# Stacked 128-row score products and single-pass sums of squares in the differential attention of a two-layer encoder

## The chip, the cores and the metric

The kernel runs on one core of one Trainium2 chip. The metric is the device time of one execution in microseconds (us). Three runs of the kernel before the change took 2218.12, 2219.3 and 2221.23 us; their median is 2219.3 us.

The engines are TensorE (PE, with its weight loads listed as PEld), VectorE (DVE), ScalarE (ACT), GpSimd (POOL) and SyncE (SP). In this kernel every data transfer is issued from SP's queue.

## What is computed

Two layers of an encoder over 512 tokens of width 1024. Each layer projects its input once and feeds three branches (a bidirectional state-space scan, differential attention, cross-attention into 256 memory tokens), gates and merges them, projects them out and normalizes. The change is in the differential attention, of which the reference says:

```python
q = _apply_rope(dq.reshape(Bsz, S, DIFF_HEADS, 2, DIFF_HEAD_DIM), cos, sin)
k = _apply_rope(dk.reshape(Bsz, S, DIFF_HEADS, 2, DIFF_HEAD_DIM), cos, sin)
...
s = jnp.einsum('bqhcd,bkhcd->bhcqk', qblk, k) * scale
p = jax.nn.softmax(s.astype(jnp.float32), axis=-1)
w = p[:, :, 0] - lam * p[:, :, 1]
return jnp.einsum('bhqk,bkhe->bqhe', w, vf)
...
o = _rmsnorm(o, diff_norm_w[layer]) * (1.0 - lambda_init)
```

There are 8 heads. Each head has two maps c of 64 channels, so a head's 128 rows of query (or key) hold map 0 in rows 0 to 63 and map 1 in rows 64 to 127. The norm at the end needs, for each token and head, the sum of squares of 128 output channels.

## The kernel before

All large products are made in float32r, a single-pass format, from operands split into a high part and a low part: `split` (line 93) copies x to the high part on ACT and subtracts it from x on DVE for the low part, and `mm3` (line 105) adds three products, low times high, high times low and high times high. Products that are given plain float32 take two passes each in the trace.

Weights come in units of 128 x 1024 (512 KB, `wr`), each loaded by one DMA and split by ACT and DVE (`emit`, line 131), two units ahead of their use. The tile framework schedules the instructions of all engines but, in the differential attention, PE: `diff` (line 793) opens a manual schedule for PE at line 984, so PE's order is the order of the text.

`diff` builds a list of units, one projection each, and lays one step per unit (lines 988 to 1016). For each head h the units are: the query of head h+1, the key of head h+1 (both `rope`, line 819), and two of the gate (`gpart`) or value (`vpart`) projections. Step s also holds, ahead of the unit's first half, the scores of query chunk s+1 (`scores`, line 873; 4 chunks of 128 tokens per head, 32 per layer) and, between the halves, the products with the values for a pair of chunks (`values`, line 907) and the turning of chunk s's weights (`turn`, line 897). In steps with s % 4 == 1 the sums of squares of the head before (`sums`, line 921) follow the scores. So a head's key is projected in the step s = 4h+1, and the first scores that read it stand at the start of step 4h+3, one step between them. The units of head 0 come before that loop; the first scores stand in the middle of `vpart(1)`.

`rope` reads the projection out of PSUM on ACT (`rx`), makes a copy with 32-row halves swapped by four DMAs of 32 rows (`rsw`, line 828), multiplies by cosine and sine and adds on DVE, and splits the result into two tiles of 128 x 512, high and low, which hold both maps.

`scores` makes three products per map on the 64 rows of that map (lines 884 to 887), the maps alternating, into two PSUM banks; DVE takes the row minimum (`fmx`; the query carries a negative scale), ACT the exponential (`fpp`).

`sums` multiplies each 128-token chunk of the squares (`sq`, float32, tile `fth`) as weights by a column of ones, four products of one column, and ACT copies the four columns to the table `ss`, tokens in rows. `norm` (line 927) makes the factors of all heads but the last after step 29, and those of the last head after step 33; `spread` and `last` distribute them, `fin` applies them and splits the result into `dy`, the operand of the branch projection. `wout` (line 1036) reuses tiles of the same pool by their tags.

## Time and profile before

One execution was profiled. It took 2223.68 us, around a span of 2221.9 us from its first to its last instruction; the mean granted TensorE clock was 0.997.

| engine | busy us | share of the span | instructions |
|---|---|---|---|
| PE | 2171.0 | 98% | 11330 |
| PEld | 1768.0 | 80% | 11330 |
| DVE | 1585.9 | 71% | 2440 |
| ACT | 1004.3 | 45% | 1895 |
| POOL | 54.2 | 2% | 38 |

A line of a timeline gives the start in us from the span's start, the duration in us, the engine, the line of the code, the operation, the tiles written and read, the shape of the array and of the operand, and the count; in brackets, how long the engine was idle before it and what it waited for. Because helpers such as `mm`, `act` and `tt` record the operations, many share a line (103, 91, 81), and the tile names tell them apart. `pm<-k,q` are the score products, `pt<-cst,fth` the sums of squares, `pj<-...` projections. A matmul is shown from its start to its modelled end; matmuls overlap, so the distance between starts is what one costs in a stream. In the list of DMAs a line gives the count, the size of each and the median time from issue to landing. The chain of waits lists, back from the last instruction, what each step waited for; its lines give start, duration and the group of instructions.

### The profile page before, as it was taken

Reading aid. Unit: us, or ns where it says so; the run is one execution under the profiler, and the core shown is the slowest. Engines: PE = TensorE matmul, PEld = TensorE weight load, DVE = VectorE, ACT = ScalarE, POOL = GpSimd, SP = SyncE. Lnnn points to the kernel's source line nnn. Section 1 sums busy time; section 2 is a strip of 40 time slices with the busy share of each in tenths; the row PEclk is TensorE's granted clock in tenths of the full one; section 3 lists DMA queues with packets and bytes.
Section 4 is the critical chain, followed back from the end, with each engine's and each line's share of the span. In section 5 each row is a group of like instructions: output and inputs, shape, how many; then the busy total and the mean of one; then the engine's idle time right before and its main releaser. Section 6 shows DMA issues by size and latency. Waiting matters only on the chain.

```text
span 2221.9 us, 29523 instructions
## 1 busy us (share of the span) xinstructions
PE 2171.0 (98%) x11330; PEld 1768.0 (80%) x11330; DVE 1585.9 (71%) x2440; ACT 1004.3 (45%) x1895; POOL 54.2 (2%) x38
## 2 busy tenths in 40 slices
PE   8999999999999999999999999999999999999998
PEld 6787877788887888878887777777788887888786
DVE  7887878758554777766467888888754547777567
ACT  5664545424442454543355564545423324554440
POOL 0000000000000000000000100000100000000000
PEclk9999999999999999999999999999999999999999
DMA  4654554425553322224564654454434333222353
GB/s 149 182 160 144 144 136 144 125 86 167 168 173 117 95 85 79 77 89 147 152 214 122 177 146 145 133 152 132 124 105 132 105 113 94 75 84 81 91 154 112
DMA packets 106162, 283.73 MB, mean 128 GB/s; under 512 B 12524, under 2 KB 13092, under 8 KB 105764
## 3 DMA queue, kind: packets, MB, share of 16 engines
q1 hardware_dynamic: 106020, 281.84, 42.4%
q8 instruction: 89, 1.46, 0.3%
q14 instruction: 53, 0.43, 0.1%
HBM read 255.55 MB, written 17.85 MB: 123 GB/s over the span
## 4 chain that ended last, share of the span: by engine, by line
PE 71%; DVE 14%; DMA 8%; ACT 5%; issue 1%; POOL 0%; SPq 0%; POOLq 0%; DVEq 0%; ACTq 0%
PE pj L103 55%; PE pm L103 13%; DMA ab<-dab 5%; DVE wl L81 3%; PE pt L111 2%; DVE ab L81 2%; DVE acc L84 2%; ACT ab L91 1%; ACT wh L91 1%; DMA wr<-wu 1%; DVE y L81 1%; DVE rx L81 1%; PE pt L103 1%; DMA fth<-rd 1%; DVE m L81 1%
## 5 line engine op out<-in xcount | busy, mean ns | idle before, releaser
L103 PE MATMUL pj<-xh,wl 128*128 128x512 f32 x1664 | 669.2, 402 | 11.0 <-DVE wl L81 8.9
L103 PE MATMUL pj<-xh,wh 128*128 128x512 f32 x1664 | 661.0, 397 | 0.0
L103 PE MATMUL pj<-xl,wh 128*128 128x512 f32 x1664 | 658.5, 396 | 0.0
L81 DVE TENSOR_TENSOR wl<-wr,wh 128x1024 fp32r<-128x1024 f32 x330 | 405.7, 1230 | 109.0 <-ACT wh L91 108.1
L91 ACT ACTIVATE wh<-wr 128x1024 fp32r<-128x1024 f32 x330 | 347.4, 1053 | 228.4 <-PE pj L103 147.4
L103 PEld LDWEIGHTS pj<-xh,wl 128*128 128x128 f32 x1664 | 313.9, 189 | 91.2 <-issue 18.3
L103 PEld LDWEIGHTS pj<-xh,wh 128*128 128x128 f32 x1664 | 313.8, 189 | 71.7 <-issue 5.7
L103 PEld LDWEIGHTS pj<-xl,wh 128*128 128x128 f32 x1664 | 314.2, 189 | 63.6 <-issue 3.6
L91 ACT ACTIVATE ab<-ab,bias 128x128 f32<-128x128 f32 x512 | 160.8, 391 | 120.5 <-DVE ab L81 119.7
L84 DVE SCALAR_TENSOR_TENSOR acc<-pj,hcw,acc 128x510 f32<-128x510 f32 x192 | 142.4, 744 | 24.2 <-ACT acc L91 22.8
L91 ACT ACTIVATE fpp<-pm,fmx 128x512 f32<-128x512 f32 x128 | 87.9, 687 | 84.3 <-DVE fmx L889 83.6
L889 DVE TENSOR_REDUCE fmx<-pm 128x1 f32<-128x512 f32 x128 | 87.0, 686 | 45.9 <-PE pm L103 45.5
L103 PE MATMUL pj<-yl,wh 128*128 128x512 f32 x256 | 102.4, 400 | 0.9 <-DVE yl L84 0.9
L103 PE MATMUL pj<-yh,wh 128*128 128x512 f32 x256 | 103.0, 403 | 0.0
L81 DVE TENSOR_TENSOR ab<-ab,cst 128x1024 f32<-128x1024 f32 x64 | 85.4, 1334 | 24.4 <-DMA ab<-dab 24.4
L103 PE MATMUL pj<-dy,wh 128*128 128x512 f32 (+1 forms) x384 | 102.2, 354 | 0.1
L103 PE MATMUL pj<-yh,wl 128*128 128x512 f32 x256 | 102.0, 399 | 0.0
L103 PE MATMUL pj<-cy,wh 128*128 128x512 f32 x256 | 78.8, 389 | 0.0
L103 PEld LDWEIGHTS pj<-dy,wh 128*128 128x128 f32 x384 | 67.8, 189 | 11.0 <-DVE dy L81 0.9
L103 PE MATMUL pj<-wh,xl 128*128 128x256 f32 x256 | 74.8, 292 | 0.0
L81 POOL TENSOR_TENSOR sqa<-sqa,sz 128x512 f32<-128x512 f32 x32 | 52.9, 1654 | 845.6 <-ACT sz L91 845.6
L103 PE MATMUL pj<-wl,xh 128*128 128x256 f32 x256 | 72.4, 283 | 0.0
(273 smaller groups left out, 3269.1 us busy)
## 6 DMA issues: line engine op xcount, KB each, us to landing
wr<-wu SPq DMA_DIRECT2D x336, 512.0 KB, 3.7
ab<-dab SPq DMA_DIRECT2D x64, 512.0 KB, 5.7
eb<-deb SPq DMA_DIRECT2D x64, 256.0 KB, 4.7
mkv<-dkv SPq DMA_DIRECT2D x16, 512.0 KB, 4.5
rsw<-rx SPq DMA_DIRECT2D x128, 64.0 KB, 2.0
dgt<-tg SPq DMA_DIRECT2D x18, 256.0 KB, 2.8
dkv<-mo SPq DMA_DIRECT2D x16, 256.0 KB, 4.2
dkv<-q SPq DMA_DIRECT2D x16, 256.0 KB, 3.6
```

What stands on the lines that cost most here:

```text
L81: (eng or self.nc.vector).tensor_tensor(out=out, in0=a, in1=b, op=op)
L84: self.nc.vector.scalar_tensor_tensor(out=out, in0=a, scalar=s, in1=b, op0=op0, op1=op1)
L91: self.nc.scalar.activation(out=out, in_=a, func=f, **kw)
L103: self.nc.tensor.matmul(out=out, lhsT=a, rhs=b, start=first, stop=last)
L111: self.nc.tensor.transpose(out=out, in_=x, identity=self.ident)
L889: nc.vector.tensor_reduce(out=mx[:, c:c + 1], in_=ps, axis=AX.X, op=ALU.min)
```

## The change

Query and key are no longer kept as high and low tiles with both maps. After the split, high and low of a head go into one tile `hl` (tag `qkh`), and DMAs lay them out anew. For the key, one tile per map holds the 64 high rows above the 64 low rows: four DMAs of 64 x 512 (128 KB). For the query, each map has a high and a low tile, each with its 64 rows twice, in both halves: four DMAs of 64 x 1024 (256 KB) into slots of a tile `qst`, two heads in turn. A score map is then two products over 128 rows, low query times key stack and high query times key stack, four per chunk in place of six over 64 rows. They include the product of both low parts, which the kernel before leaves out.

For the sums, the squares are split into high and low (tile `sqs`). Two products with weights `pick` of 8 columns, whose column h is ones for head h and zero otherwise, give a result of 8 x 512 with the sums in row h, which DVE adds to `sr`. Before each `norm`, a new step `flip` turns the four chunks of `sr` with four transposes and copies the heads needed to `ss`.

To find room, `qst` and `sqs` take the slots of `dy`, which is allocated anew in a step `room` after step 32; some tags of `wout` change with it. A constant of 64 columns is added.

```diff
+            hl = self.t(fp, [P, 2, S], "qkh", F32R)
+            self.split(hl[:, 0, :], hl[:, 1, :], x)
+            half = [slice(64 * c, 64 * c + 64) for c in range(2)]
+            if nm == "q":
+                o = [self.qst[:, 4 * (h % 2) + 2 * c:4 * (h % 2) + 2 * c + 2, :] for c in range(2)]
+                self.qk[h, nm] = [[t[:, i, :] for i in range(2)] for t in o]
+                parts = [(o[c][r], hl[half[c]]) for c in range(2) for r in half]
+            else:
+                o = self.qk[h, nm] = [self.t(fp, [P, S], f"k{c}", F32R) for c in range(2)]
+                parts = [(o[c][half[i], :], hl[half[c], i, :]) for c in range(2) for i in range(2)]
+            for to, src in parts:
+                nc.sync.dma_start(out=to.bitcast(F32), in_=src.bitcast(F32))
...
-            for n, (a, b) in enumerate(((ql, kh), (qh, kl), (qh, kh))):
-                for c in range(2):
-                    rows = slice(64 * c, 64 * c + 64)
-                    self.mm(pss[c], a[rows, qs], b[rows, :], n == 0, n == 2)
+            for c in range(2):
+                (qh, ql), k = self.qk[h, "q"][c], self.qk[h, "k"][c]
+                self.mm(pss[c], ql[:, qs], k, True, False)
+                self.mm(pss[c], qh[:, qs], k, False, True)
...
-                self.sq = self.t(self.fp, [P, S], "fth")
-                self.act(self.sq, po, AF.Square)
+                sq = self.t(self.fp, [P, S], "fth")
+                self.act(sq, po, AF.Square)
+                self.sq = [self.sqs[h % 2][:, i, :] for i in range(2)]
+                self.split(*self.sq, sq)
...
         def sums(h):
             pt = self.bank(self.pt, "pt")
+            for i in (1, 0):
+                self.mm(pt[:KC], self.pick[:, h, :], self.sq[i], i == 1, i == 0)
+            if h == 0:
+                self.act(self.sr, pt[:KC])
+            else:
+                self.tt(self.sr, self.sr, pt[:KC], ALU.add)
+
+        def flip(lo, hi):
+
+            pt = self.bank(self.pt, "pt")
             for c in range(4):
-                self.mm(pt[:, c:c + 1], self.sq[:, c * P:(c + 1) * P], self.ones[:, 0:1])
-            self.act(self.ss[:, 4 * h:4 * h + 4], pt[:, 0:4])
+                nc.tensor.transpose(out=pt[:, c * KC:(c + 1) * KC], in_=self.sr[:, c * P:(c + 1) * P],
+                                    identity=self.ident[:KC, :KC])
+            self.act(self.ss[:, 4 * lo:4 * hi].rearrange("p (h c) -> p h c", c=4),
+                     pt[:, :4 * KC].rearrange("p (c h) -> p h c", c=4)[:, lo:hi])
...
             if s in (nst - 3, nst + 1):
+                self.T(job(flip, *((0, KC - 1) if s < nst else (KC - 1, KC))))
                 self.T(job(norm, *((0, KC - 1) if s < nst else (KC - 1, KC))))
+            if s == nst:
+                self.T(room)
```

## The prediction

> **What bounds the kernel now.** I read the page first: the engines' busy time, then the chain of work that ended last.

> ```profile
> PE 2171.0 (98%) x11330; PEld 1768.0 (80%) x11330; DVE 1585.9 (71%) x2440; ACT 1004.3 (45%) x1895; POOL 54.2 (2%) x38
> PE 71%; DVE 14%; DMA 8%; ACT 5%; issue 1%; POOL 0%; SPq 0%; POOLq 0%; DVEq 0%; ACTq 0%
> ```

> TensorE (PE) is busy nearly all the time and carries 71% of the chain, so PE time removed shows in the total wherever nothing else is late. The change sits in the differential-attention stage, where the chain leaves PE once per head. The timeline of one such place, the key of head 3 in layer 0, with the DMA queue's own lines:

> ```profile
> 818.71 0.60 ACT L91 ACTIVATE rx<-pj 128x512 f32<-128x512 f32 x1 [2.16 <-PE pj L103]
> 819.33 2.41 SPq L828 DMA_DIRECT2D rsw<-rx  x4
> 821.42 0.68 DVE L81 TENSOR_TENSOR q<-rx,q 128x512 fp32r<-128x512 f32 x1
> 823.95 0.68 DVE L81 TENSOR_TENSOR rx<-rx,cos 128x512 f32<-128x512 f32 x1
> 826.53 0.63 ACT L91 ACTIVATE k<-rx 128x512 fp32r<-128x512 f32 x1 [1.50 <-DVE rx L81]
> 826.79 0.39 PE L103 MATMUL pj<-xh,wh 128*128 128x512 f32 x1
> 827.19 0.69 DVE L81 TENSOR_TENSOR k<-rx,k 128x512 fp32r<-128x512 f32 x1
> 827.94 0.73 PE L103 MATMUL pm<-k,q 64*128 64x512 f32 x4 [0.22 <-DVE k L81]
> 828.60 0.51 PE L103 MATMUL pj<-xh,wl 128*128 128x512 f32 x1
> ```

> The projection of the key ends, ACT reads it out at 818.71, the half-swap goes through DMA from 819.33, VectorE (DVE) rotates it, ACT and DVE split it into high and low at 826.53 and 827.19. The score products of the next head wait for that: DVE is done at 827.19 + 0.69 = 827.88, four of the six products start at 827.94. PE is already the one that waits: from 826.79 to 828.60 are 1.81 us, where a block that doesn't wait (below) has 1.22, so 0.6. There is no slack behind the key's split: whatever is put between the split and the products delays PE by its full length.

> **The score products themselves.** A block whose operands are there, on PE's timeline:

> ```profile
> 834.23 0.39 PE L103 MATMUL pj<-xl,wh 128*128 128x512 f32 x1
> 834.45 0.39 PE L103 MATMUL pj<-xh,wh 128*128 128x512 f32 x1
> 834.77 0.97 PE L103 MATMUL pm<-k,q 64*128 64x512 f32 x6
> 835.67 0.50 PE L103 MATMUL pj<-xh,wl 128*128 128x512 f32 x1
> 836.00 0.40 PE L103 MATMUL pj<-xl,wh 128*128 128x512 f32 x1
> ```

> Full products follow each other every 0.23 us (834.23 to 834.45). From the last one before the block (834.45) to the second one behind it (836.00) are 1.55 us, of which two steps of 0.23 would pass anyway: the block costs 1.09 us. Six products of 0.23 would be 1.38, so the two 64-row halves do run beside each other in pairs, and entering and leaving that form eats part of the gain. The new block is four full products, 4 x 0.23 = 0.92 us: 0.17 saved. Not the third that a count of six against four suggests.

> Of the 64 blocks, 16 are the first of a head and are costed with the stall below. In 14 intervals (heads 1 to 7, two layers) one more block lies between the end of the key's projection and the stalled products; time saved there only lengthens the wait, as the key's chain starts at the projection's end. That leaves 34 x 0.17 = 5.8 us.

> **The sums of squares.**

> ```profile
> 810.34 0.39 PE L103 MATMUL pj<-xh,wh 128*128 128x512 f32 x1
> 810.66 0.96 PE L103 MATMUL pm<-k,q 64*128 64x512 f32 x6
> 811.55 1.05 PE L103 MATMUL pt<-cst,fth 128*128 128x1 f32 x8
> 812.46 0.48 PE L103 MATMUL pj<-xh,wl 128*128 128x512 f32 x1
> 812.78 0.39 PE L103 MATMUL pj<-xl,wh 128*128 128x512 f32 x1
> ```

> Each of the four full-precision products makes two passes (8 records). From 810.34 to 812.78 are 2.44 us; less 0.46 and the block of 1.09, the sums take 0.89. Their replacement is two products of 512 columns with 8 weight columns. Nothing that narrow is in the trace; the nearest has 64 weight columns:

> ```profile
> 26.99 0.39 PE L103 MATMUL pj<-xh,wh 128*128 128x512 f32 x1
> 27.21 0.40 PE L103 MATMUL pj<-xh,yl 128*64 128x512 f32 x1
> 27.45 0.39 PE L103 MATMUL pj<-xl,yl 128*64 128x512 f32 x1
> ```

> It enters at the normal step (0.22, 0.24), so I take 0.46 for the two: 0.43 saved. If entering and leaving cost what the score block pays beyond its three pairs (1.09 - 0.69 = 0.40), nothing is saved. 16 heads: -6.9 us, between 0 and -6.9.

> The flips are new: four calls, each with four small transposes. A group of four costs this in the chain:

> ```profile
> 782.66 0.44 PE pt L111 x4
> ```

> 4 x 0.44 = +1.8 us. They come a step after the sums, with half a step left before their result is used.

> New work on ACT and DVE: per head a split of the squares (0.63 and 0.69, the sizes of the key's split above) and an addition of 8 rows by 512 columns on DVE, at most the 0.69 of a 128-row one, in place of a small copy on ACT. It falls into the two steps with the longest waits for PE:

> ```profile
> 810.76 0.60 ACT L91 ACTIVATE rx<-pj 128x512 f32<-128x512 f32 x1 [2.13 <-PE pj L103]
> 811.65 0.69 DVE L889 TENSOR_REDUCE fmx<-pm 128x1 f32<-128x512 f32 x1 [2.13 <-PE pm L103]
> ```

> Idle times of 2.13 us on both cover it: nothing. Were that cover gone, DVE's 1.38 us per head would come to 22 us.

> **The stacking, which is the price.** Products over 128 rows need high and low of one map above each other, that is, data moved across partitions. Per head the change adds four DMAs of 128 KB behind the key's split and four of 256 KB behind the query's, all in SP's queue.

> ```profile
> L828 SPq DMA_DIRECT2D rsw<-rx x128: 507/588/598, 721.8 to 2056.4; - x128
> wr<-wu SPq DMA_DIRECT2D x336, 512.0 KB, 3.7
> eb<-deb SPq DMA_DIRECT2D x64, 256.0 KB, 4.7
> rsw<-rx SPq DMA_DIRECT2D x128, 64.0 KB, 2.0
> dab<-eb SPq DMA_DIRECT2D x2, 128.0 KB, 3.1
> ```

> Issue: 0.59 us each, as the swap. Landing of 128 KB: 2.0 us is the swap's (SBUF to SBUF, half the bytes), 3.1 that of 64 rows of 2 KB to DRAM (the same bytes); far ends are 2.0 and, for 256 KB, 4.7. I take the middle of the two near rows, 2.55.

> For head 3: the first part (high, map 0) needs only ACT's half and goes at 827.16; the second (low, map 0) waits for DVE and goes at 827.88, the third at 828.47, the fourth at 829.06, and lands at 831.61. Map 0's two products run meanwhile; map 1's two take 0.46, and the projection goes on at 832.07 where it went on at 828.60: +3.47 us per head. Behind the waiting products on PE stand all projections, in an order written by hand, so nothing fills the hole.

> The first head of a layer has more room before its products, yet they too start as the split ends:

> ```profile
> 734.64 0.69 DVE L81 TENSOR_TENSOR k<-rx,k 128x512 fp32r<-128x512 f32 x1
> 735.20 0.92 PE pm L103 x6
> 736.12 3.07 PE pj L103 x24
> ```

> The split ends at 735.33, the fourth part goes at 736.51 and lands at 739.06; +0.46 is 739.52 against 736.12: +3.4. Sum: 14 x 3.47 + 2 x 3.4 = +55.4 us.

> The query's parts wait for its split (821.42 + 0.68 = 822.10), hold SP until 824.5 and are due only with the key's: they cost nothing beside it, unless their 1 MB is still moving when the key's parts go (then the 4.7 end). Next weights were asked for before them, two steps ahead of use. [...]

> **Sum.** 55.4 - 5.8 - 6.9 + 1.8 = +44.5 us. The profiled execution took 2223.7 us around its span of 2221.9 (so 2268.2 by the same profile); the median of the runs is 2219.3, hence **2263.8 us**.

> **The rivals.**

> *Hidden (faster).* The key could be stacked in time if its chain started earlier. What is to be had: the swap's last part, issued at about 821.1, has landed by 823.1 and its product waits in DVE's order until 823.95; between that and the split stand other DVE operations of some 1.4 us. Even 2.2 us recovered and a landing of 2.0 leave 3.47 - 0.55 - 2.2 = 0.7 us per head, 11.5 in all, against 10.9 saved (5.8 + 6.9 - 1.8): the sign turns only below 0.7 us per head. Fully hidden, with today's waits of 0.6 gone as well, 2219.3 - 10.9 - 14 x 0.17 - 14 x 0.6 gives 2198. Chance 0.08; against it speaks that the parts' own issue and landing are longer than all of this slack.

> *The query's parts ahead of the key's swap.* In the program the query's stacking stands before the key's swap. If SP keeps that order, the swap goes at 824.5 instead of 819.33, some 5 us later, and so does the key: 14 x 5 more, about 2334. Against it: the swap was ready at 819.33, the query's split ended at 822.10, and ACT already does the key's readout (818.71) ahead of the query's split. Chance 0.1.

> *The slow clock.* After a long wait PE runs at half pace for a while:

> ```profile
> 6.89 0.77 PE L103 MATMUL pj<-xh,wl 128*128 128x512 f32 x1 [6.89 <-DVE wl L81]
> 10.55 0.43 PE L103 MATMUL pj<-xh,wh 128*128 128x512 f32 x1
> 15.70 0.50 PE L103 MATMUL pj<-xh,wl 128*128 128x512 f32 x1 [1.30 <-DVE wl L81]
> 16.04 0.39 PE L103 MATMUL pj<-xl,wh 128*128 128x512 f32 x1
> ```

> Behind 6.89 us of waiting, eight steps took 3.66 us instead of 1.84; behind 1.30 us none was slow. The new hole is 827.02 (826.79 + 0.23) to 830.43, when map 0's second part lands: 3.4 us, between the two. If it counts as long, 16 x 1.8 = +29 us: 2293. [...] Chance 0.2.

> *Nothing.* A stall of just 0.7 us per head would cancel the savings: 2219, chance 0.04.

> **How the numbers follow.** My case, 0.58; clock 0.2; query first 0.1; hidden 0.08; nothing 0.04. With a landing of 2.0 and 1.5 us of DVE's slack recovered the stall is 1.4 us and the time 2231; with 4.7 it is 5.6 and the time 2298; with a landing of 3.95 and the clock's price on top, 2315. The range is 2228 to 2315: it leaves out hidden, nothing and most of query first. Within 0.2% is about what a measurement can tell from no change. Faster 0.08, same 0.04, slower 0.88.

> **What would show it.** In the profile after: score products of 128 rows in blocks of 0.92 us; ahead of the first block of each head PE idle of about 3 us put down to the DMAs of the key's stack, and some 55 us of such waits in all; sums in 0.46 us; the swap still issued ahead of the query's parts; projections behind the hole at steps of 0.23 (mine) or 0.46 (clock). Waits of PE on the key's DMAs below 1 us per head would prove me wrong, and point to DVE's order.

## The result and the profile after

The changed kernel takes 2301.35 us, the median of four runs (2299.27 to 2303.7), against 2218.71 us for the kernel before on the same chip (2217.99 to 2221.23). The ratio is 1.0371, with a 95% interval of 1.0356 to 1.0387: slower by 82.6 us, where the prediction said 44.5. The profiled execution took 2303.7 us, and its mean granted clock was 0.975 (before: 0.997).

From the page after: the busy times, the group of the score products (busy time, mean ns of one | idle time before them and what ended most of it), and the DMAs of the key's parts (KB each, median us from issue to landing).

```profile
PE 2198.6 (96%) x11122; PEld 1807.1 (79%) x11122; DVE 1609.8 (70%) x2470; ACT 1007.7 (44%) x1903; POOL 52.7 (2%) x38
L103 PE MATMUL pm<-k,dy 128*128 128x512 f32 x256 | 87.0, 461 | 60.6 <-DMA k<-qkh 59.7
k<-qkh SPq DMA_DIRECT2D x64, 128.0 KB, 2.5
```

PE has 208 instructions fewer, and yet it is busy 27.6 us longer: some of what it does goes at a slower pace. And it now stands idle for 59.7 us ahead of score products whose key stack has not landed. The next fence shows where: the timeline of after at the key of head 3 in layer 0, the place that the prediction showed of before.

```profile
831.36 2.41 SPq L836 DMA_DIRECT2D rsw<-rx  x4
834.29 3.13 SPq L853 DMA_DIRECT2D dy<-qkh  x4
838.67 0.39 PE L103 MATMUL pj<-xh,wh 128*128 128x512 f32 x1
838.94 0.63 ACT L91 ACTIVATE qkh<-rx 128x512 fp32r<-128x512 f32 x1 [2.02 <-DVE rx L81]
839.59 2.46 SPq L853 DMA_DIRECT2D k<-qkh  x4
842.62 1.19 PE L103 MATMUL pm<-k,dy 128*128 128x512 f32 x2 [3.56 <-DMA k<-qkh]
843.99 1.19 PE L103 MATMUL pm<-k,dy 128*128 128x512 f32 x2 [0.18 <-issue]
844.98 0.63 PE L103 MATMUL pj<-xh,wl 128*128 128x512 f32 x1
845.40 0.63 PE L103 MATMUL pj<-xl,wh 128*128 128x512 f32 x1
...
848.34 0.39 PE L103 MATMUL pj<-xh,wh 128*128 128x512 f32 x1
```

The last projection product starts at 838.67; the next one that isn't a score product starts at 844.98. Less one step of 0.23 that is a span of 6.08 us; the same place of before had 1.58. In it: the split, four issues in 2.46 us, the wait of 3.56 us, and four products at about half pace (the last two take 0.99 us, 843.99 to 844.98, in place of 0.46). Behind it eight projection steps go at up to 0.43 us (844.98 to 845.40 is one; all eight, to 848.34, take 3.36 us, where eight steps of 0.23 are 1.84) before the pace returns.

The first head of a layer has it worse. First the DMA queue's lines and the products of layer 0, then the key's parts in the DMA view of 724 to 738 us:

```profile
726.71 3.52 SPq L853 DMA_DIRECT2D dy<-qkh  x4
730.36 3.78 SPq L853 DMA_DIRECT2D k<-qkh  x4
737.30 2.37 PE L103 MATMUL pm<-k,dy 128*128 128x512 f32 x4 [5.75 <-DMA k<-qkh]
```

```profile
k<-qkh SPq DMA_DIRECT2D x4, 128.0 KB, 5.0
```

Here the query's 1 MB leaves just ahead of the key's parts, both move at once (in this view the query's four parts, issued from 726.71 to 730.23, take 6.3 us to land), and the key's take 5.0 us to land instead of 2.5. The same view has two weight units of 512 KB under way; which of the two loads slows the key's parts isn't separated. The 3.78 us of the four issues hold a wait: the first part goes 1.66 us ahead of the second, which needs DVE's half of the split.

A block that waits for nothing, with the sums behind it:

```profile
860.79 1.09 PE L103 MATMUL pm<-k,dy 128*128 128x512 f32 x4
861.72 0.62 PE L103 MATMUL pt<-dy,pick 128*8 128x512 f32 x2
862.17 0.39 PE L103 MATMUL pj<-xh,wl 128*128 128x512 f32 x1
862.40 0.40 PE L103 MATMUL pj<-xl,wh 128*128 128x512 f32 x1
```

The block takes 0.93 us (860.79 to 861.72), the sums 0.45 (to 862.17), and the step behind is the normal one. So both products became cheaper on PE, as meant.

The loss lies in the differential attention. From the first readout of a query to the issue of the write of the first seven heads' factors (`rd<-rt`) it took 269.0 and 268.9 us in the two layers; now 308.9 and 309.6, together +80.6.

### The profile page after: what moved, and what is told of

Read it like the earlier page. It is cut to its first block, busy times and chain, and to the rows that moved or that the text cites. A ratio compares the mean times of both kernels' runs of the same rounds, so it can differ in the third digit from the quotient of the medians.

```text
span 2301.9 us, 29444 instructions
## 1 busy us (share of the span) xinstructions
PE 2198.6 (96%) x11122; PEld 1807.1 (79%) x11122; DVE 1609.8 (70%) x2470; ACT 1007.7 (44%) x1903; POOL 52.7 (2%) x38
## 3 DMA queue, kind: packets, MB, share of 16 engines
q8 instruction: 87, 1.43, 0.3%
## 5 line engine op out<-in xcount | busy, mean ns | idle before, releaser
L103 PE MATMUL pj<-xh,wl 128*128 128x512 f32 x1664 | 668.8, 402 | 10.2 <-DVE wl L81 8.5
L103 PE MATMUL pj<-xh,wh 128*128 128x512 f32 x1664 | 665.3, 400 | 0.0
L103 PE MATMUL pj<-xl,wh 128*128 128x512 f32 x1664 | 663.6, 399 | 0.0
L81 DVE TENSOR_TENSOR wl<-wr,wh 128x1024 fp32r<-128x1024 f32 x330 | 404.4, 1226 | 107.7 <-ACT wh L91 107.2
L91 ACT ACTIVATE wh<-wr 128x1024 fp32r<-128x1024 f32 x330 | 347.2, 1053 | 222.5 <-PE pj L103 149.6
L103 PEld LDWEIGHTS pj<-xh,wl 128*128 128x128 f32 x1664 | 317.4, 191 | 82.3 <-ACT xh L91 7.0
L103 PEld LDWEIGHTS pj<-xh,wh 128*128 128x128 f32 x1664 | 316.7, 190 | 72.2 <-issue 5.7
L103 PEld LDWEIGHTS pj<-xl,wh 128*128 128x128 f32 x1664 | 317.3, 191 | 67.1 <-issue 3.6
L91 ACT ACTIVATE ab<-ab,bias 128x128 f32<-128x128 f32 x512 | 160.7, 391 | 115.0 <-DVE ab L81 114.1
L103 PE MATMUL pm<-k,dy 128*128 128x512 f32 x256 | 87.0, 461 | 60.6 <-DMA k<-qkh 59.7
L91 ACT ACTIVATE fpp<-pm,fmx 128x512 f32<-128x512 f32 x128 | 87.3, 686 | 92.2 <-DVE fmx L906 92.0
L103 PEld LDWEIGHTS pm<-k,dy 128*128 128x128 f32 x256 | 50.3, 213 | 81.0 <-issue 45.3
L103 PE MATMUL pj<-yl,wh 128*128 128x512 f32 x256 | 102.8, 402 | 0.8 <-DVE yl L84 0.8
L103 PE MATMUL pj<-dy,wh 128*128 128x512 f32 (+1 forms) x384 | 102.7, 356 | 1.0 <-DVE dy L81 1.0
L103 PE MATMUL pj<-yh,wh 128*128 128x512 f32 x256 | 103.2, 403 | 0.0
L103 PE MATMUL pj<-yh,wl 128*128 128x512 f32 x256 | 102.7, 402 | 0.0
L81 DVE TENSOR_TENSOR ab<-ab,cst 128x1024 f32<-128x1024 f32 x64 | 86.7, 1355 | 19.7 <-DMA ab<-dab 19.6
L103 PE MATMUL pj<-wh,xl 128*128 128x256 f32 x256 | 79.1, 309 | 0.0
L103 PE MATMUL pj<-cy,wh 128*128 128x512 f32 x256 | 78.8, 389 | 0.0
L103 PEld LDWEIGHTS pj<-dy,wh 128*128 128x128 f32 x384 | 67.5, 188 | 13.4 <-DVE dy L81 2.3
## 6 DMA issues: line engine op xcount, KB each, us to landing
wr<-wu SPq DMA_DIRECT2D x336, 512.0 KB, 3.7
ab<-dab SPq DMA_DIRECT2D x64, 512.0 KB, 5.3
eb<-deb SPq DMA_DIRECT2D x64, 256.0 KB, 4.9
dy<-qkh SPq DMA_DIRECT2D x64, 256.0 KB, 4.1
mkv<-dkv SPq DMA_DIRECT2D x16, 512.0 KB, 4.2
k<-qkh SPq DMA_DIRECT2D x64, 128.0 KB, 2.5
dgt<-tg SPq DMA_DIRECT2D x18, 256.0 KB, 2.8
```

Source lines behind the costliest of these rows:

```text
L81: (eng or self.nc.vector).tensor_tensor(out=out, in0=a, in1=b, op=op)
L91: self.nc.scalar.activation(out=out, in_=a, func=f, **kw)
L103: self.nc.tensor.matmul(out=out, lhsT=a, rhs=b, start=first, stop=last)
```

## The experiments

Theory A, the prediction's: the stack is late, so PE waits once per head; each hole costs what the split, the issues and the landing add. Theory B adds the slow clock: behind a hole of this length PE runs at half pace for some steps. Of the parts of the change, the sums were held to be a small gain, and the work on ACT and DVE free.

### One part alone

`s1_sums_only` has the new sums and the old scores and rotation:

```diff
-                (qh, ql), k = self.qk[h, "q"][c], self.qk[h, "k"][c]
-                self.mm(pss[c], ql[:, qs], k, True, False)
-                self.mm(pss[c], qh[:, qs], k, False, True)
+            for n, (a, b) in enumerate(((ql, kh), (qh, kl), (qh, kh))):
+                for c in range(2):
+                    rows = slice(64 * c, 64 * c + 64)
+                    self.mm(pss[c], a[rows, qs], b[rows, :], n == 0, n == 2)
```

> The kernel before with the new sums of squares alone (split squares, two products of 512 columns per head, flip); score products as before. My theory: two products at 0.23 us for the 0.89 us of the four double-pass ones, 16 heads, plus four flips of 0.44: 2218.7 - 6.9 + 1.8 = 2213.6 us. Rival, entering and leaving the 8-column form costs what the score block pays (0.40): 2218 to 2221. Rival, the split and the addition on ACT and DVE are not covered: up to 22 us more, 2236. Then a part of the 82 us would lie here.

Measured: 2232.12 us, 1.005 of before (1.0038 to 1.0063). A miss: +11 instead of -5, and inside the bounds of the last rival, that the split and the addition are not covered. Of the profiled run's +8.6, the two stages hold +3.9 (270.9 us each against 269.0 and 268.9); the rest lies in stages that the change doesn't touch, where small waits come and go between profiles, and I give it no cause. Inside the stage the sums do cost PE half of what they did, but the span of the first block now is longer at heads 2 to 7 (2.25, 2.48, 2.19, 2.47, 2.20 and 2.07 us in layer 0; before 1.30, 1.58, 1.29, 1.58, 1.29 and 1.75). That is 4.9 us a layer, 9.8 for both, against 16 x 0.43 = 6.9 saved: most of the +3.9. The timeline of one such head (5), and then the same instructions in before (head 4; from readout to split all heads from 1 to 6 take 7.82 or 7.83 us there):

```profile
881.66 0.60 ACT L91 ACTIVATE rx<-pj 128x512 f32<-128x512 f32 x1 [2.15 <-PE pj L103]
887.20 0.75 DVE L84 SCALAR_TENSOR_TENSOR fpp<-fpp,fsm 128x512 f32<-128x512 f32 x1
887.87 0.69 DVE L81 TENSOR_TENSOR rx<-rx,cos 128x512 f32<-128x512 f32 x1
890.38 0.63 ACT L91 ACTIVATE k<-rx 128x512 fp32r<-128x512 f32 x1 [2.40 <-DVE rx L81]
```

```profile
851.34 0.60 ACT L91 ACTIVATE rx<-pj 128x512 f32<-128x512 f32 x1 [2.15 <-PE pj L103]
856.59 0.69 DVE L81 TENSOR_TENSOR rx<-rx,cos 128x512 f32<-128x512 f32 x1
857.79 0.75 DVE L84 SCALAR_TENSOR_TENSOR fpp<-fpp,fsm 128x512 f32<-128x512 f32 x1
859.17 0.63 ACT L91 ACTIVATE k<-rx 128x512 fp32r<-128x512 f32 x1 [1.41 <-DVE rx L81]
```

From the key's readout to its split are 8.72 us (881.66 to 890.38) against 7.83. The order of DVE's queue has changed: the softmax's `fpp` now stands ahead of the key's `rx<-rx,cos`, where it stood behind it. The issue of the swap also took longer here (3.72 against 2.41 us), but that doesn't decide: at the other nine places of heads 2 to 6 it takes 2.41 us, and the split is as late (8.72 to 8.77 us), each time with `fpp` ahead. It is the order.

`s2_stack_only` is the changed kernel with the old sums and no flip:

```diff
-            for i in (1, 0):
-                self.mm(pt[:KC], self.pick[:, h, :], self.sq[i], i == 1, i == 0)
+            for c in range(4):
+                self.mm(pt[:, c:c + 1], self.sq[:, c * P:(c + 1) * P], self.ones[:, 0:1])
```

> The changed kernel with the sums of squares as before; only the stacking and the 128-row products remain. My theory: the loss is all in the stacking, so 2301.4 + 5 = 2306 us, with holes ahead of each head's first products as long as in the changed kernel. Rival, the sums cause a part of the loss: well below 2301.

Measured: 2300.36 us, 1.036 (1.0344 to 1.0375). The stacking holds the whole loss, and the sums bring nothing in the changed kernel. The spans of the 16 stalled blocks are 90.4 us in all here, 93.2 with the new sums, and the slow steps behind them 1.35 us here against 1.58 on average, where the projection behind has 512 columns. Only a part of that is a later key: over the 14 later heads the split starts 0.08 us later on average with the new sums, 1.2 us in all. The rest is pace, and whether a hole brings the slow pace depends on where it lies in time (below), so this isn't shown to be the sums' doing.

### The clock

`w14_warm_hole` puts 14 products of 512 columns, whose result nobody reads, ahead of the first score block of each head, so that PE works while the stack is under way:

```diff
+            if qc == 0:
+                d = self.bank(self.pm, "pm")
+                for i in range(14):
+                    self.mm(d, self.xh[:, i % KC, :P], self.xh[:, i % KC, :])
```

> The changed kernel with 14 extra full products (3.2 us, result unused) on TensorE ahead of each head's first score products, where it waits for the key's stack; the wait itself is left as it is. Theory of two causes (wait plus slow clock behind it): the products behind the hole go at steps of 0.23 instead of 0.43, so 16 x (1.6 + 0.4) = 32 us less: 2269 us (2262 to 2280). Rival, the wait alone: the filled hole changes nothing, 2301 us, or more if the extra products run over.

Measured: 2276.28 us, 1.0256 (1.0235 to 1.0277). More work, 25 us less (27 if each is set against the kernel before that was measured beside it): theory B. The timeline at head 3:

```profile
835.22 3.33 PE L103 MATMUL pm<-xh 128*128 128x512 f32 x14
838.64 0.71 PE L103 MATMUL pm<-k,dy 128*128 128x512 f32 x2
...
840.19 0.39 PE L103 MATMUL pj<-xh,wl 128*128 128x512 f32 x1
```

Two score products take 0.71 us instead of 1.19, and the first projection product behind them 0.39 instead of 0.63. The granted clock is 0.996.

`w7_half_warm` has seven of these products, to leave a hole of some 2 us:

```diff
-                for i in range(14):
+                for i in range(7):
```

> The changed kernel with 7 extra full products (1.6 us) ahead of each head's first score products, so that some 1.6 to 2.1 us of waiting remain in each hole. If the clock falls only after a longer idle time than that, the time is that of the fully filled holes, about 2269 us. If any hole of 2 us brings the slow steps back: 2301 us.

Measured: 2290.65 us, 1.032 (1.0304 to 1.0335): between the two expectations, so neither holds. Two heads of this one profile show why (heads 1 and 7 of layer 0):

```profile
773.44 0.71 PE L103 MATMUL pm<-k,dy 128*128 128x512 f32 x2 [1.77 <-DMA k<-qkh]
774.44 1.02 PE L103 MATMUL pm<-k,dy 128*128 128x512 f32 x2 [0.29 <-issue]
775.26 0.63 PE L103 MATMUL pj<-xh,wl 128*128 128x512 f32 x1
...
990.26 0.71 PE L103 MATMUL pm<-k,dy 128*128 128x512 f32 x2 [1.61 <-DMA k<-qkh]
991.47 0.70 PE L103 MATMUL pm<-k,dy 128*128 128x512 f32 x2 [0.50 <-issue]
992.01 0.40 PE L103 MATMUL pj<-xh,wl 128*128 128x512 f32 x1
```

```profile
771.21:774.63 3.42, 1.37 (x6) 1.00 0.88 199
774.63:778.04 3.41, 3.41 (x9) 0.50 0.68 258
986.25:989.66 3.41, 2.40 (x11) 1.00 0.90 226
989.66:993.08 3.42, 2.32 (x9) 1.00 0.95 268
993.08:996.49 3.41, 3.41 (x19) 1.00 0.27 109
```

At head 1 the whole hole lies within one stretch, in which PE is busy for 1.37 us, and in the next the granted clock is 0.50. At head 7 a boundary cuts the hole in two, PE is busy for 2.40 and 2.32 us, and the clock stays at 1.00. The attention stages of the 13 traces hold some 2000 such stretches at full clock. Every one with PE busy for less than 1.5 us was followed by one at half clock, and none with more than 1.7 us; between these both occur. In the changed kernel all 16 holes brought half clock, behind stretches with 0.00 to 1.40 us of work; no other stretch of its attention stages has less than 1.88. These are counts of the attention stages alone: elsewhere in after, stretches with 1.93 us (from 1189.59) and 2.20 us (from 448.90) had half clock behind them too.

### Issue order of the key's parts

`o1_part_order` issues both high parts first, which need only ACT's half of the split, and then both low ones:

```diff
-                    parts = [(o[c][half[i], :], hl[half[c], i, :]) for c in range(2) for i in range(2)]
+                    parts = [(o[c][half[i], :], hl[half[c], i, :]) for i in range(2) for c in range(2)]
```

> The changed kernel with the key's four DMAs in another order: both high parts, which need only ACT's half of the split, then both low parts. Theory: the issue of the parts one behind the other is on the path; two instead of three follow the end of the split, so the last lands 0.59 us sooner: -9.4 us in 16 heads, 2292 us; with holes shorter by that much fewer reach the limit of the clock, which can give up to 25 us more (2267). Rival, the parts are held up by the bytes in front of them (the query's 1 MB): no change, 2301 us.

Measured: 2312.85 us, 1.0416 (1.0402 to 1.043), another miss: slower by 11 us (9 against the kernel before that was measured beside it), not faster. My working was wrong: DVE's half comes only 0.7 us behind ACT's, while four issues take 2.46 us, so the queue, not the split, sets when the last part leaves, in either order. And map 0 needs its low part, which now goes third instead of second, so its two products no longer run while map 1's parts are under way. The holes of layer 0 are 3.7 to 4.6 us (first head 7.7), where after has 3.0 to 3.7 (first head 5.75).

### An earlier key

If the stack is merely late, the cure is to project the key earlier. `r0_early_before` is the kernel before, and `r1_early_after` the whole change, with query and key moved up one unit, behind which the other units follow (a gate unit that had shared a step moves too):

```diff
+        step(rope(1, "q"), (), ())
...
-                units += [rope(h + 1, "q"), rope(h + 1, "k")]
+                units.append(rope(h + 1, "k"))
...
+                if h + 2 < KC:
+                    units.append(rope(h + 2, "q"))
```

> The kernel before with another order of its units: the query and the key of each later head are projected one step sooner (the query of head 1 before the values of head 0), and one gate goes from the scan stage into this stage to keep the number of steps. Theory: the waits of about 0.5 us for 14 keys go, -7 to -8 us: 2211 us, or up to 4 more if the scan stage misses the gate as filling.

> The changed kernel with the same order of units. Each key now has two steps (some 15 us) instead of one for its split and its stack. My theory: the loss was the wait for the key's stack and the clock behind it, so both go; what stays is the gain of the products, 64 x 0.13 + 6.9 - 1.8 = 13 us below the kernel before in this order: 2198 us, clock near 0.997. Rival, the stacking costs by itself (queue, bandwidth, or products of 128 rows): not below the other order's time, 2211 or more, and up to 2290 if the loss has nothing to do with the wait.

Measured: `r0_early_before` 2212.77 us, 0.997 of before (0.996 to 0.998), as expected. `r1_early_after` 2254.11 us, 1.0151 (1.0137 to 1.0165): 47 us better than the change, but 56 above what I expected. Holes of 2 us stay at nearly every head. The DMA queue's timeline says why, with the products of that head:

```profile
886.79 1.14 SPq L836 DMA_DIRECT2D rsw<-rx  x2
888.03 3.19 SPq L853 DMA_DIRECT2D dy<-qkh  x4
891.28 2.46 SPq L836 DMA_DIRECT2D rsw<-rx  x2
...
904.23 1.33 PE L103 MATMUL pm<-k,dy 128*128 128x512 f32 x4 [2.03 <-DMA k<-qkh]
```

Two of the key's four swap DMAs stand behind the four that stack the query. That is the prediction's rival "the query's parts ahead of the key's swap", which did not occur in the changed kernel itself and does occur here. Behind most of these holes the clock stays up (0.994 over the run; four of them brought half clock).

`r2_swap_first` puts the query's parts further back in SP's queue, by a lower priority:

```diff
+                with self.late(100 if nm == "q" else 0):
+                    for to, src in parts:
+                        nc.sync.dma_start(out=to.bitcast(F32), in_=src.bitcast(F32))
```

> The whole change with query and key one unit earlier (r1_early_after), and the query's four stacking DMAs put behind the key's swap in SP's queue; nothing else differs. Theory (in r1_early_after the query's parts stood between the two halves of the key's swap, four issues of 3.19 us on the path of the key's chain): the key's parts leave some 3.2 us earlier, more than the 2.0 us that its products still waited, so no hole is left at the heads after the first; 16 spans of 3.2 to 3.8 us go to 0.93, about -42 us on 2254: expected 2210 us (2203 to 2220), no wait of the score products for DMA k<-qkh but at the first head, clock 0.997. Rival (the chain of the key is late for another reason, the rotated order or the four issues of its own parts): holes of 2 us stay, 2248 to 2256 us.

`r3_swap_first_old_sums` is the same without the new sums.

> As r2_swap_first, with the heads' sums of squares as in the kernel before, so that only the stacking is left of the change. Theory (the new sums save what the prediction gave them once no wait covers it, 0.43 us a head): r2_swap_first plus 7 us, 2217. Rival (the sums save nothing on the path, as the same times of s2_stack_only and the whole change say): within 3 us of r2_swap_first. Third (the sums cost, as in s1_sums_only): 5 to 11 us under r2_swap_first.

Measured: `r2_swap_first` 2223.26 us, 1.0019 (1.001 to 1.0028), and `r3_swap_first_old_sums` 2218.09 us, 0.9996 (0.9987 to 1.0005). Of the holes, only those of the first heads are left, and one of 0.6 us at the second; SP's order was the cause. But r2 stands 13 us above its expectation, and r3 is 5 us under r2: the third case of its expectation, the sums cost. From r2 and then from r3, the timeline around the sums:

```profile
843.93 0.69 DVE L81 TENSOR_TENSOR dy<-fth,dy 128x512 fp32r<-128x512 f32 x1 [0.89 <-ACT dy L91]
845.28 1.09 PE L103 MATMUL pm<-k,dy 128*128 128x512 f32 x4
845.80 0.68 DVE L81 TENSOR_TENSOR wT<-pt,wT 128x512 fp32r<-128x512 f32 x1
846.54 0.64 PE L103 MATMUL pt<-dy,pick 128*8 128x512 f32 x2 [0.16 <-DVE wT L81]
847.01 0.28 PE L103 MATMUL pj<-wh,xl 128*128 128x256 f32 x1
```

```profile
842.41 0.68 DVE L81 TENSOR_TENSOR wT<-pt,wT 128x512 fp32r<-128x512 f32 x1
843.51 1.10 PE L103 MATMUL pm<-k,dy 128*128 128x512 f32 x4
844.44 0.95 PE L103 MATMUL pt<-cst,fth 128*128 128x1 f32 x8
845.25 0.37 PE L103 MATMUL pj<-wh,xl 128*128 128x256 f32 x1
```

In r2 the sums' products are put down to DVE's `wT<-pt,wT`, the reader of a PSUM tile of the same pool as the sums' result. It ends at 846.48, and they start at 846.54; in r3 it was done at 843.09, before the block. In r2 DVE has the split of the squares (`dy<-fth,dy`) in its queue, which itself waits 0.89 us for ACT. From the block's end (845.28 + 0.93 = 846.21) to the next projection at 847.01 the sums then take 0.80 us, against 0.81 for the old ones (844.44 to 845.25). All that the cheaper products save is spent waiting on DVE, here and at 12 of the 14 heads whose sums follow a block: block and sums take 1.70 us on average in r2 and 1.75 in r3. What makes r2 the slower one lies elsewhere: in the flips (0.4 to 0.5 us each in after), and at the first two heads of the layers, where the blocks are 1.1 us longer in all and the slow steps behind the first ones 2.4; no run ties the last two to the sums.

The stacked scores do pay once they are in time: with the old sums, two heads take 63.21 us in r3 (from the block at 780.30 to that at 843.51) and 64.41 us in r0 (777.40 to 841.81), 0.6 us a head. What r3 loses again lies at the first heads, whose first block waits for the query's parts (spans of 5.46 and 4.15 us against 0.88 in r0). So `r4_swap_first_but_head0` leaves the first query's parts where they were:

```diff
-                with self.late(100 if nm == "q" else 0):
+                with self.late(100 if nm == "q" and h else 0):
```

> As r3_swap_first_old_sums (stacking alone, query and key one unit earlier, the query's four parts behind the key's swap), but the first query's parts go without being put back, since in r3 the first score block of a layer waited 3.7 us for DMA dy<-qkh (span 5.46 and 4.15 us in place of 0.88), and 2.2 and 1.6 us in r1_early_after. Theory: the stacking then is almost fully hidden, and what it is worth on TensorE shows: about 62 blocks at 0.93 in place of 1.06 us, -8, less some 3 us for the two first heads and 1 for the second ones: 5 us under r0 (2207 if r0 is 2212). Rival (the work that moves to SP's queue, ACT and DVE delays other work of the stage by as much as the blocks gain): within 3 us of r0 or above it, 2212 to 2218.

> The kernel before with query and key one unit earlier, once more, beside r4_swap_first_but_head0 on one chip. As r0_early_before: 0.997 of the kernel before, 2212 to 2214 us.

Measured: `r4_swap_first_but_head0` 2214.53 us, 0.9981 (0.9971 to 0.9991), and `r0_again` 2212.66 us, 0.9967 (0.9957 to 0.9977). The rival holds: within 2 us. The first block's span fell to 2.22 and 1.65 us, but the wait moved to the second head, whose key stack is now late:

```profile
759.32 0.39 PE L103 MATMUL pj<-xh,wh 128*128 128x512 f32 x1
761.69 1.34 PE L103 MATMUL pm<-k,dy 128*128 128x512 f32 x4 [1.98 <-DMA k<-qkh]
762.88 0.40 PE L103 MATMUL pj<-xh,wl 128*128 128x512 f32 x1
```

The span from 759.32 + 0.23 to 762.88 is 3.33 us, 2.4 more than without a wait. In the two stages together r4 is 1.8 us shorter than r0 (269.5 and 269.7 us against 270.5 and 270.5), too little to show in the total. The fastest version found is r0: the kernel before, with query and key projected one unit earlier and nothing of the change.

## Why the prediction was right about the sign and short on the size

The direction and the main mechanism held: score products of 128 rows at 0.93 us (0.92 predicted), PE idle ahead of the first block of each head, put down to the key's stack, 59.7 us (some 55 predicted), the swap issued ahead of the query's parts. The parts' issue (2.46 us for four) and landing (2.5 us, 2.55 predicted) were right too, the landing with some luck: it was the middle between rows of 2.0 and 3.1. The total was short by 38 us. The measured time lies in the upper part of the range, which the prediction reached by a landing of 3.95 us at every head with the clock's price on top; the clock came at every head, the longer landing at the first heads alone. The steps, by the profile after; each line is the difference to the profile before:

| step | predicted us | measured us |
|---|---|---|
| stalled blocks, heads 1 to 7 of both layers | 14 x 3.47 = +48.6 | 14 x 3.97 = +55.6 |
| stalled blocks, first heads | 2 x 3.4 = +6.8 | +7.07 and +7.96 = +15.0 |
| slow steps behind the holes | 0 | about +21 |
| free blocks | 34 x 0.17 = -5.8 | 48 x 0.13 = -6.2 |
| sums | -6.9 | -6.9 on PE alone |
| flips | +1.8 | 2 x 0.42 + 2 x 0.53 = +1.9 |
| both stages | +44.5 | +80.6 |

**The stall** was sized too small by 0.5 us a head, and that is the slow clock again. The prediction took the key's split where the trace of before had it, and full pace for the products. The first held at most heads: the waits ahead of the 14 later blocks are 3.3 us on average (3.4 predicted), and at eleven of the 14 heads the split starts no later than before. The second didn't: at head 3 the last two products take 0.99 us (843.99 to 844.98) instead of 0.46, which is 0.53 too much. Head 3 itself, predicted +3.47 and measured 6.08 - 1.58 = +4.50, is one of the three with a later split besides (the others are head 6 of both layers): it starts 0.27 us behind the last projection product (838.94 against 838.67), where before it started 0.26 ahead (826.53 against 826.79).

**The first heads.** The prediction gave them the landing of the others, and named the case that the query's 1 MB could still be moving. At the first head of layer 0 the key's parts take 5.0 us to land while that 1 MB and two weight units are under way, and the last of them is issued 1.88 us behind the split's end, where 1.18 was taken.

**"It counts as long" was a rival with a chance of 0.2, and it came true on top of the main case.** Its price, 16 x 1.8 = 29 us, was about right: `w14_warm_hole` gains 25 us. The 21 of the table is what is left of the 80.6 when the other lines are taken off; the half-paced score products, 14 x 0.5 = 7 us, are counted in the stalled blocks. Eight of the 16 heads could be measured directly: 0.68 to 2.00 us of slow steps, 1.58 on average. The failed step is the reading that a hole of 3.4 us lies "between the two" and probably doesn't count; the chance of 0.2 was the author's estimate, and in the changed kernel all 16 holes brought half clock. `w7_half_warm` shows what the reading left out: the clock changes at points 3.41 us apart, and it fell behind a stretch in which PE was still busy for 1.37 us, but not behind two with 2.40 and 2.32 us, with holes of about 2.1 us in both places. A hole of 3.4 us takes at least half of one of the stretches that it touches, wherever it lies.

**"Covers it: nothing" failed for the new work on ACT and DVE.** The rows of 2.13 us of idle time were real, but idle time covers work only if the work falls there. `s1_sums_only` shows the key's split coming 0.9 us later behind its readout (8.72 us against 7.83), and `r2_swap_first` shows PE waiting for a reader that stands later in DVE's order (done at 846.48, in `r3_swap_first_old_sums` at 843.09). r2 is 5 us slower than r3, where the new sums, flips taken off, should have saved 5; the wait explains that they save nothing, not the whole of the 5. In the changed kernel they came out at nothing (2301.35 with, 2300.36 without).

**The rivals.** "Hidden" did not occur: only moved up a unit and with SP's queue in order do r3 and r4 show it nearly so, at 2214 to 2218 us, not the 2198 computed, which had no wait left at the first heads and took the sums' gain as whole. "The query's parts ahead of the key's swap" was rightly seen as a danger and rightly thought absent here; it came with the rotation.

What stays open: the 5 us by which the stages outside the attention differ between the profiles of before and of `s1_sums_only`; what slows the landing at the first heads; and what decides on the clock where PE is busy for 1.5 to 1.7 us of a stretch.

## What to carry to other kernels

A product saved on a busy engine is worth less than the step that lays out its operands, if that step stands at the end of a chain that already ends just in time (here 0.13 us a free block against 3.97 us a stalled one): price the whole chain, its issues one after the other, and the hole's consequences (the clock) with it. Idle time of an engine is cover only where the new instruction really stands (here 2.13 us idle in a step, and a key's split 0.9 us late all the same); read the queue's order after the change, not the sum of its gaps. When a layout step needs time, move its producer earlier first and look at every queue that the move passes: here the move alone gave 0.997, and the stacking added nothing to it (0.998).

## What the runs showed of the hardware that was not expected

- In the attention stages of these traces the length of PE's idle time did not by itself say whether the clock fell; PE's busy time between two of the points 3.41 us apart did (half clock always followed below 1.5 us and never above 1.7). Behind the hole of 1.98 us shown above (`r4_swap_first_but_head0`, second head; PE busy for 1.65 us from 758.06 to 761.48) the next projection product takes 0.40 us, as everywhere at full pace; behind one of 1.98 us at the same head of `r1_early_after` (busy for 1.43 us from 760.18 to 763.59) it takes 0.63 (at 764.70).
- Filling a hole with useless products made the kernel 25 us faster (`w14_warm_hole`, 2276.28 us against 2301.35).
- Products with only 8 weight columns go at the step of full ones (0.45 us for two, and 0.23 for the step behind): no price for entering or leaving that form shows, unlike for the pairs of 64 rows of before, where three pairs cost 1.09 us and three steps of 0.23 would be 0.69.
